# Another order of units in the mixers of a two-block decoder, and half of the low parts moved to VectorE

## Chip, core and metric

The kernel runs on one core of one Trainium2 chip. The metric is the device time of one execution in microseconds (us), lower is better. TensorE does the matrix products, VectorE, ScalarE and GpSimd the elementwise work, SyncE issues the weight loads. In the profile they are PE, DVE, ACT, POOL and SP.

## What is computed

Input is one sequence of 512 positions of width 1024. Two blocks follow each other. The first holds two attention layers (one with a forget gate, one with a sliding window of 128 and sinks). The second block, in which the change lies, is cut here to its core:

```python
h = rmsnorm_2(x, norm_mix_w) * (1.0 + sc1) + sh1
proj = h @ w_in
(hq, hf, hi, hg, sq, sk, sv, iq, ik, iw, cu) = split(proj)
o_a = hgrn2_mixer(hq, hf, hi, hg, lower_bounds, onorm_w)   # 4 heads, 128 x 128, gated linear recurrence
o_b = dsa_mixer(sq, sk, sv, iq, ik, iw)                    # 4 heads of 64, softmax over the 128 best keys
o_c = conv_module(cu, cv_w, cv_b, ln_w, ln_b)              # gated, 31 taps over positions, layer norm, swish
x = x + g1 * (concatenate([o_a, o_b, o_c]) @ w_out)
h = rmsnorm_2(x, norm_mlp_w) * (1.0 + sc2) + sh2
x = x + g2 * (square(relu(h @ mlp_w1)) @ mlp_w2)
return rmsnorm_2(x, final_norm_w)
```

All of it is in float32. The three mixers `hgrn2_mixer`, `dsa_mixer` and `conv_module` depend on nothing of each other until the product with `w_out`.

## The kernel before

**Products.** Positions lie in four tiles of 128. A float32 product is three products of a reduced format (`mm3`, L270 to L275): every operand is a high part and a low part. A weight group is 1024 x 512, loaded in four quarters `raw` of 128 x 1024 (`load_group`, L248 to L268; the pool has three `raw` buffers, so the load of a quarter waits until the one three before it is done with). ScalarE writes the high part `wh` (L259), and the low part `wl = raw - wh` comes from GpSimd for the quarters listed in `gpl` and from VectorE otherwise (L259, recorded at helper line L115). A product over a quarter needs both.

**Units.** The mixers are emitted by a hand-written list of units, `ORDER` (L1160), one word each; words that repeat run a generator from one `yield` to the next. The words: `iq` and `sv` project the indexer's queries and the sparse values (groups narrower than 512); `s1` to `s3` are indexer scores of a position tile (`score`, L833: eight products `Si`, each ReLU on ScalarE, then a sum `sct` on VectorE), `t1` to `t3` select the 128 best keys (`select`, L852: 16 MAX and 15 MATCH_REPLACE rows on VectorE, then the mask `posm`); `f0`, `f1` and `v0`, `v1` are gates (`hg_gates`, L908) and values (`hg_values`, L935: products `pshi`, gate `thg`) for heads 0 and 1 or 2 and 3; `h0` to `h3` are the four linear-recurrence heads (`hg_head`, L956); `cu` and `c0`, `c1` are the convolution's projection and its two halves (`u_cv`, L1119: one row and 30 taps `cv` each on VectorE); `sqk` projects the sparse queries and keys; `d0`, `d1` are the two pairs of sparse-attention heads (`u_dsa`, L1111, with `fox_pair`); `ln` is the convolution's layer norm.

**A head.** `hg_head` multiplies halves of ever longer runs of positions: a first block product, `D`, and nine levels (`lev` 0 to 8). A level is a product `psA` on TensorE, a masked copy into `D` on VectorE (L998, levels 0 to 5), and then doubling (L980): `qv` times `prod` or `kG` on VectorE, `kG` times `prod` on GpSimd, before the next level's product. Each needs the one before. Then come the output product `Oh`, a normalisation with a root on GpSimd (`hhr`), ScalarE's scaling `on`, a transpose `pth` and the mixer output `xm`.

**What sets the order.** Words are emitted in the order of the list; a static scheduler then fixes one instruction order per engine at build time, taking earlier words first where several instructions could run. On the chip each engine works through its list in order and waits by semaphore. Buffers are shared by tag: seven of 128 x 512 (`w2`, used by `rsi`, `E`, `sg`, `prod`, `D`, `gt`, `eq`, `pre` and more), three banks `mm` for large products, two `ss` for `Si`, `psA` and the sparse scores `S`.

Behind the list, `residual` (L638) multiplies the mixer outputs with `wo2`.

Of the kernel before, what the change touches and what calls it, by code (L numbers as in the profile page):

```python
# [64 lines left out]
def decoder_kernel(ctx: ExitStack, tc: tile.TileContext, a: dict, out: bass.AP, upto="all"):  # L65
# [750 lines left out]
    levm = const.tile([128, 6, 64], U8, name="levm")  # L816
    ve.tensor_copy(levm, levf.rearrange("p (l j) -> p l j", j=64))

    gpc = [int(x) for x in "0123"]
    gpo = [int(x) for x in "0"]  # L820
    cnt[1] = int("1000")
    LAG = "v"
# [334 lines left out]
            stt(zz, th, 1.0, zz, ALU.add, ALU.mult)  # L1157
            mix_out(1, 2 + m, zz, 0.5)

    ORDER = "iq sv s2 s3 f0 f0 f0 s1 v0 v0 t2 f1 f1 f1 cu h1 h1 t3 h0 h1 h0 c1 sqk h1 h0 t1 sqk h0 v1 d1 d1 d1 d1 d1 d0 v1 d0 d0 d0 c0 h2 h2 h2 ln h3 d0 h3 h3 h2 h3".split()  # L1160
    gens = {}

    def unit(w):
# [10 lines left out]

    for w in ORDER:
        k, n = w[0], int(w[1]) if w[1].isdigit() else None
# [222 lines left out]
```

## Time and profile before

| | |
|---|---|
| Time, median of 3 runs | 1336.72 us (1330.08 to 1338.33) |
| The profiled execution | 1335.75 us, span 1334.0 us |
| TensorE busy, whole span | 1232.4 us (92%) |
| VectorE busy, whole span | 819.5 us (61%) |
| ScalarE busy, whole span | 550.6 us (41%) |
| GpSimd busy, whole span | 312.0 us (23%) |
| Low parts on VectorE, whole span | 104 of 128 x 1024, 129.7 us |
| Low parts on GpSimd, whole span | 34, 76.4 us |

Times in the trace count from the start of the span. The mixers lie between about 646 and 931. A row of the timeline gives start, duration, engine, line, operation, the tile written and the tiles read, and in brackets how long the engine was idle ahead of it and which instruction ended that. A stretch's busy time counts an instruction that is held up on the way as busy.

### The profile page before, as it was taken

What the parts mean: (1) busy time and instruction counts of PE and PEld (TensorE: products, weight loads), DVE (VectorE), ACT (ScalarE), POOL (GpSimd) and SP (SyncE); (2) the same over time, 40 slices, a digit from 0 to 9 for tenths busy, and PEclk for the clock granted to TensorE, in tenths of its full rate; (3) what the DMA queues carried; (4) which work ended last, traced back from release to release, by engine and by line L of the source; (5) the groups of instructions that cost most, each with busy time, mean ns of one, the idle gap of its engine ahead of it and who ended that gap; (6) DMA issues with size and microseconds to landing.
All of it is one profiled execution on the core that took longest, in us unless ns stands there. A gap on an engine that the chain in (4) does not pass through costs nothing.

```text
span 1334.0 us, 17842 instructions
## 1 busy us (share of the span) xinstructions
PE 1232.4 (92%) x6596; PEld 1008.0 (76%) x6596; DVE 819.5 (61%) x1598; ACT 550.6 (41%) x1144; POOL 312.0 (23%) x362
## 2 busy tenths in 40 slices
PE   5999998999999989999988896878999999999997
PEld 4677777878886878888776665766788888888886
DVE  4647656756467678545699979863675244353444
ACT  4544453554255657526433134613352322131222
POOL 1304302210124240003335634142111010015211
PEclk9999999999999889999999999888999999999999
DMA  5234324423532343252322302120364233234221
GB/s 200 66 112 142 127 81 157 143 66 126 204 107 69 95 142 127 66 182 93 98 67 79 111 1 67 48 80 17 110 206 158 89 117 108 82 116 153 95 79 64
DMA packets 42023, 141.72 MB, mean 106 GB/s; under 512 B 4928, under 2 KB 5824, under 8 KB 41936
## 3 DMA queue, kind: packets, MB, share of 16 engines
q1 hardware_dynamic: 36144, 126.06, 29.2%
q10 hardware_dynamic: 5792, 14.52, 3.1%
q8 instruction: 52, 0.85, 0.3%
q14 instruction: 35, 0.29, 0.1%
HBM read 132.14 MB, written 8.42 MB: 105 GB/s over the span
## 4 chain that ended last, share of the span: by engine, by line
PE 54%; DVE 11%; issue 8%; POOL 6%; DMA 2%; ACT 2%; POOLq 0%; SPq 0%; ACTq 0%; DVEq 0%
PE psw L275 4%; PE psw L274 4%; PE psw L273 4%; PE psf L275 4%; PE psf L274 4%; PE psf L273 4%; POOL wl L115 3%; PE pso L274 2%; PE pso L273 2%; PE pso L275 2%; DVE cv L118 2%; PE psg L275 2%; PE psg L274 2%; PE psg L273 2%; PE Ob L743 2%
## 5 line engine op out<-in xcount | busy, mean ns | idle before, releaser
L259 ACT ACTIVATE wh<-raw 128x1024 fp32r<-128x1024 f32 (+2 forms) x138 | 142.3, 1037 | 164.8 <-PE psw L275 50.5
L115 DVE TENSOR_TENSOR wl<-raw,wh 128x1024 fp32r<-128x1024 f32 x104 | 129.7, 1260 | 58.5 <-ACT wh L259 56.3
L115 POOL TENSOR_TENSOR wl<-raw,wh 128x1024 fp32r<-128x1024 f32 (+2 forms) x34 | 76.4, 2264 | 83.0 <-ACT wh L259 82.9
L274 PE MATMUL psf<-xfl,wh 128*128 128x512 f32 (+1 forms) x232 | 85.4, 369 | 0.5 <-DVE xfl L118 0.5
L275 PE MATMUL psf<-xfh,wl 128*128 128x512 f32 (+1 forms) x232 | 85.3, 368 | 0.3 <-DVE wl L115 0.2
L115 POOL TENSOR_TENSOR hnr<-hnr,mhalf 128x8 f32<-128x8 f32 (+1 forms) x28 | 49.6, 1771 | 153.5 <-DVE hnr L111 148.2
L273 PE MATMUL psf<-xfh,wh 128*128 128x512 f32 (+1 forms) x232 | 84.5, 368 | 0.0
L1239 POOL TENSOR_SCALAR acth<-sqf 128x512 fp32r<-128x512 f32 x32 | 22.9, 718 | 242.3 <-DVE sqf L115 242.3
L273 PE MATMUL psw<-wh,acth 128*128 128x512 f32 (+1 forms) x206 | 79.0, 383 | 0.0
L275 PE MATMUL psw<-wh,actl 128*128 128x512 f32 (+1 forms) x206 | 78.9, 383 | 0.0
L274 PE MATMUL psw<-wl,acth 128*128 128x512 f32 (+1 forms) x206 | 78.9, 383 | 0.0
L519 ACT ACTIVATE PT<-ptp 128x512 f32<-128x512 f32 (+3 forms) x96 | 45.5, 481 | 43.0 <-PE ptp L548 30.2
L336 DVE CUSTOM_DVE_ANT_0 adaw<-adaw,cact 128x1024 f32<-128x1024 f32 x48 | 58.1, 1225 | 7.1 <-DMA adaw<-in_ada 6.9
L511 ACT ACTIVATE P<-Sp,nm 128x128 f32<-128x128 f32 (+3 forms) x80 | 44.5, 557 | 28.2 <-DVE nm L509 27.9
L118 DVE SCALAR_TENSOR_TENSOR cv<-glu,cols,cv 128x482 f32<-128x482 f32 (+29 forms) x60 | 55.5, 930 | 0.4
L273 PE MATMUL psq<-wh,xah 128*128 128x512 f32 x128 | 54.0, 422 | 0.8 <-ACT xah L294 0.8
L275 PE MATMUL psq<-wh,xal 128*128 128x512 f32 x128 | 53.4, 417 | 0.2 <-DVE xal L115 0.2
L274 PE MATMUL psq<-wl,xah 128*128 128x512 f32 x128 | 52.8, 413 | 0.0
L275 PEld LDWEIGHTS psf<-xfh,wl 128*128 128x128 f32 x232 | 43.7, 188 | 8.2 <-DVE wl L115 1.1
L274 PEld LDWEIGHTS psf<-xfl,wh 128*128 128x128 f32 x232 | 43.7, 188 | 8.1 <-DVE xfl L118 0.9
L273 PEld LDWEIGHTS psf<-xfh,wh 128*128 128x128 f32 x232 | 43.5, 188 | 7.3
L554 PEld LDWEIGHTS O<-v,PT 128*128 128x128 f32 x320 | 42.8, 193 | 7.5 <-ACT PT L519 5.1
(501 smaller groups left out, 3471.5 us busy)
## 6 DMA issues: line engine op xcount, KB each, us to landing
raw<-in_w SPq DMA_DIRECT2D x56, 512.0 KB, 3.7
adaw<-in_ada SPq DMA_DIRECT2D x48, 512.0 KB, 4.2
raw<-in_wa SPq DMA_DIRECT2D x32, 512.0 KB, 4.6
raw<-in_w2m SPq DMA_DIRECT2D x32, 512.0 KB, 4.0
raw<-in_wb SPq DMA_DIRECT2D x16, 512.0 KB, 4.7
ck<-cd ACTq DMA_DIRECT2D x16, 256.0 KB, 4.1
raw<-in_woa SPq DMA_DIRECT2D x8, 512.0 KB, 4.7
raw<-in_wob SPq DMA_DIRECT2D x8, 512.0 KB, 4.7
```

The lines of the kernel that those rows point to most:

```text
L115: return note(eng, eng.tensor_tensor(o, x, y, op=op))
L118: return note(ve, ve.scalar_tensor_tensor(o, x, s, y, op0=op0, op1=op1, **kw))
L259: i = ac.activation(wh, r, AF.Copy), tt(gp if len(res) in (gpa if gpl is None else gpl) else ve, wl, r, wh.bitcast(F32), ALU.subtract)
L273: te.matmul(o, lh, rh, start=i == 0, stop=False)
L274: te.matmul(o, lh, rl, start=False, stop=False)
L275: te.matmul(o, ll, rh, start=False, stop=i == n - 1)
L336: i = ve.tensor_tensor_reduce(w, w, ada["c"], 1.0, 0.0, op0=ALU.mult, op1=ALU.add, accum_out=mod[:, j:j + 1])
L511: ac.activation(P[:, :n], Sp[:, :n], AF.Exp, bias=nm, scale=-1.0, accum_out=l)
L519: ac.activation(o, i, AF.Copy)
L554: te.matmul(O[:, i, s], PT[s][:, j], v[:, j, (2 * p + s) * 64:(2 * p + s + 1) * 64], start=j == 0, stop=j == i)
L743: te.matmul(O[:, i, s], PTs[s, kb][:, i], vb[:, n - nkb + 1 + kb, g * 64:g * 64 + 64], start=kb == 0, stop=kb == nkb - 1)
L1239: gp.tensor_scalar(xh, s, 1.0, 0.0, op0=ALU.mult, op1=ALU.add)
```

## The change

Two constants. `gpc` is the `gpl` of all eight weight groups of the mixers: quarters 0 and 2 stay on GpSimd, quarters 1 and 3 go to VectorE. `ORDER` lists the same words (the same units, each as often as it has pieces) in another order.

```diff
-    gpc = [int(x) for x in "0123"]
+    gpc = [int(x) for x in "02"]
...
-    ORDER = "iq sv s2 s3 f0 f0 f0 s1 v0 v0 t2 f1 f1 f1 cu h1 h1 t3 h0 h1 h0 c1 sqk h1 h0 t1 sqk h0 v1 d1 d1 d1 d1 d1 d0 v1 d0 d0 d0 c0 h2 h2 h2 ln h3 d0 h3 h3 h2 h3".split()
+    ORDER = "iq sv s2 s1 f0 f0 f0 v0 v0 t2 h1 s3 f1 h0 f1 f1 t1 cu h0 c1 sqk h1 h1 h0 h0 sqk h1 t3 v1 d1 d0 d1 d1 d1 c0 d0 d0 v1 h2 d0 h2 h3 ln h2 h3 h2 d0 h3 d1 h3".split()
```

What this does to the engines' lists is shown at three places. The first is VectorE at the end of the first value group and the selection of tile 2 (`gt`, `eq`, `pre` of scores `sct_6195`). Before:

```order
L868 TENSOR_SCALAR gt_6672,cg_6675<-sct_6195,m8_6670 128x384
L118 SCALAR_TENSOR_TENSOR thg_6620<-thg_6620,pshi_6594 128x256
L111 TENSOR_SCALAR eq_6673<-sct_6195,m8_6670 128x384
L112 TENSOR_SCALAR need_6679<-cg_6675 128x1
L862 MAX m8_7070<-sct_6239 128x8
L870 SCALAR_TENSOR_TENSOR pre_6674<-ones1_106,eq_6673 128x384
L864 MATCH_REPLACE sct_6239<-m8_7070,sct_6239 128x512
L118 SCALAR_TENSOR_TENSOR eq_6673<-pre_6674,need_6679,eq_6673 128x384
L862 MAX m8_7073<-sct_6239 128x8
L115 TENSOR_TENSOR gt_6672<-gt_6672,eq_6673 128x384
L864 MATCH_REPLACE sct_6239<-m8_7073,sct_6239 128x512
```

Now:

```order
L868 TENSOR_SCALAR gt_6628,cg_6631<-sct_6195,m8_6626 128x384
L118 SCALAR_TENSOR_TENSOR thg_6576<-thg_6576,pshi_6550 128x256
L111 TENSOR_SCALAR eq_6629<-sct_6195,m8_6626 128x384
L112 TENSOR_SCALAR need_6635<-cg_6631 128x1
L115 TENSOR_TENSOR qv_6308<-qv_6308,kG_6307 128x512
L870 SCALAR_TENSOR_TENSOR pre_6630<-ones1_106,eq_6629 128x384
L115 TENSOR_TENSOR D_6650<-psA_6652,idc_5849 128x256
L118 SCALAR_TENSOR_TENSOR eq_6629<-pre_6630,need_6635,eq_6629 128x384
L998 COPY_PREDICATED D_6650<-levm_5851,psA_6663 128x256
L115 TENSOR_TENSOR gt_6628<-gt_6628,eq_6629 128x384
L115 TENSOR_TENSOR qv_6308<-qv_6308,kG_6307 128x256
L115 TENSOR_TENSOR wl_6762<-raw_6759,wh_6761 128x1024
```

The first rows and levels of head 1 (`D`, `qv`) now stand in that selection, where rows of the next selection stood, and the fourth low part of the second gate group (`wl_6762`) follows on VectorE.

The second place is the loading of the second value group (`raw_7616` to `raw_7634`, unit `v1`). Before, all four of its low parts stood on GpSimd:

```order
L115 TENSOR_TENSOR hhr_7398<-hhr_7398,mhalf_104 128x4
L115 TENSOR_TENSOR kG_6307<-kG_6307,prod_7117 128x128
L115 TENSOR_TENSOR wl_7619<-raw_7616,wh_7618 128x1024
L115 TENSOR_TENSOR wl_7625<-raw_7622,wh_7624 128x1024
L115 TENSOR_TENSOR wl_7631<-raw_7628,wh_7630 128x1024
L115 TENSOR_TENSOR wl_7637<-raw_7634,wh_7636 128x1024
```

Now the second and fourth stand on VectorE, here:

```order
L118 SCALAR_TENSOR_TENSOR cv_7174<-glu_7031,cols_84,cv_7174 128x509
L115 TENSOR_TENSOR qv_6308<-qv_6308,prod_6801 128x128
L118 SCALAR_TENSOR_TENSOR cv_7174<-glu_7031,cols_84,cv_7174 128x510
L864 MATCH_REPLACE sct_6697<-m8_7587,sct_6697 128x512
L118 SCALAR_TENSOR_TENSOR cv_7174<-glu_7031,cols_84,cv_7174 128x511
L862 MAX m8_7590<-sct_6697 128x8
L115 TENSOR_TENSOR wl_7625<-raw_7622,wh_7624 128x1024
L115 TENSOR_TENSOR on_7411<-Oh_7400,gg_6433 128x512
L864 MATCH_REPLACE sct_6697<-m8_7590,sct_6697 128x512
L115 TENSOR_TENSOR wl_7637<-raw_7634,wh_7636 128x1024
```

They follow the last of the 30 taps of one half of the convolution (`cv`, 511 columns), among which the last levels of heads 0 and 1 (`qv`) and the selection of tile 3 (`sct_6697`) are spread.

The third place is VectorE behind the last tap. `D_8084` and `D_8036` belong to head 2, `D_8266` and `D_8177` to head 3; `qv_6709` and `qv_6766` hold the queries of both. Before, the end of head 2 and the start of head 3:

```order
L115 TENSOR_TENSOR qv_6709<-qv_6709,kG_6708 128x512
L112 TENSOR_SCALAR ct_8189<-ptc_8190,bmv_8205,rrcr_8207 128x256
L112 TENSOR_SCALAR ct_8189<-ptc_8211,bmv_8218,rrcr_8220 128x256
L1144 BN_STATS bst_8224<-ptc_8211 128x6
L115 TENSOR_TENSOR qv_6709<-qv_6709,kG_6708 128x256
L1146 BN_AGGR bmv_8226<-bst_8224 128x2
L111 TENSOR_SCALAR rrcr_8228<-bmv_8226 128x1
L112 TENSOR_SCALAR ct_8189<-ptc_8211,bmv_8226,rrcr_8228 128x256
L118 SCALAR_TENSOR_TENSOR zz_8237<-th_8239,zz_8237 128x512
L115 TENSOR_TENSOR D_8266<-psA_8268,idc_5849 128x256
```

Now:

```order
L998 COPY_PREDICATED D_8036<-levm_5851,psA_8133 128x256
L115 TENSOR_TENSOR qv_6766<-qv_6766,prod_8026 128x32x8
L559 RECIPROCAL rl8f_8121<-l8f_7729 128x8
L115 TENSOR_TENSOR onf_8123<-O_7728,rl8f_8121 128x512
L998 COPY_PREDICATED D_8036<-levm_5851,psA_8145 128x256
L115 TENSOR_TENSOR qv_6766<-qv_6766,prod_8026 128x16x16
L1144 BN_STATS bst_8230<-ptc_8225 128x6
L1146 BN_AGGR bmv_8232<-bst_8230 128x2
L115 TENSOR_TENSOR xm_7867<-O_7728,xm_7866 128x512
L998 COPY_PREDICATED D_8036<-levm_5851,psA_8157 128x256
L115 TENSOR_TENSOR D_8177<-psA_8179,idc_5849 128x256
L115 TENSOR_TENSOR qv_6766<-qv_6766,kG_6765 128x512
```

Head 3's `D` stood behind all nine levels of head 2 and the layer norm's tiles `ct`; it now stands behind head 2's level 5, and the end of a sparse pair (`onf_8123`, `xm_7867`) stands ahead of it, behind the last tap.

## Rows read from the trace of the kernel before

**Rows 1.** Busy time by stretch, mixers; columns in the first line.

```profile
core 0: us, PE busy (x) PEld busy (x) DVE busy (x) ACT busy (x) POOL busy (x), PEclk, DMA share, GB/s
646.20:758.30 112.10, 99.17 (x426) 76.47 (x426) 108.93 (x195) 41.79 (x66) 50.26 (x34) 0.98 0.26 81
758.30:833.20 74.90, 57.59 (x448) 44.60 (x447) 64.64 (x109) 25.40 (x62) 36.38 (x39) 0.94 0.18 52
833.20:880.10 46.90, 41.78 (x268) 34.61 (x269) 39.14 (x78) 24.44 (x64) 11.22 (x17) 0.91 0.26 87
880.10:931.40 51.30, 40.03 (x329) 30.53 (x328) 23.16 (x56) 15.43 (x45) 16.83 (x28) 0.85 0.02 8
```

**Rows 2.** Timeline, TensorE, 823.6 to 834; start, us, line, tiles, [idle before, releaser].

```profile
823.62 0.40 PE L273 MATMUL pshi<-wh,xch 128*128 128x512 f32 x1
823.85 0.40 PE L274 MATMUL pshi<-wl,xch 128*128 128x512 f32 x1
...
833.74 0.77 PE L1038 MATMUL pth<-ident,on 128*128 128x128 f32 x2 [9.50 <-ACT on L1035]
```

**Rows 3.** Groups by form, VectorE, 640-930; busy us, mean ns, idle us before.

```profile
L118 DVE SCALAR_TENSOR_TENSOR sct<-rsi,siw,sct 128x384 f32<-128x384 f32 x7 | 8.2, 1172 | 0.7
...
L111 DVE TENSOR_SCALAR kG<-sg 128x512 f32<-128x512 f32 x4 | 6.4, 1589 | 0.0
...
L118 DVE SCALAR_TENSOR_TENSOR kG<-E,oml,sg 128x512 f32<-128x512 f32 x4 | 5.2, 1290 | 0.0
...
L115 DVE TENSOR_TENSOR wl<-raw,wh 128x1024 fp32r<-128x1024 f32 x3 | 3.6, 1215 | 0.0
...
L118 DVE SCALAR_TENSOR_TENSOR cv<-glu,cols,cv 128x503 f32<-128x503 f32 x2 | 1.5, 739 | 0.0
```

**Rows 4.** Timeline around the second value group's low parts: GpSimd, then VectorE.

```profile
804.94 10.71 POOL L115 TENSOR_TENSOR wl<-raw,wh 128x1024 fp32r<-128x1024 f32 x4 [1.92 <-ACT wh L259]
...
804.99 2.88 DVE L118 SCALAR_TENSOR_TENSOR cv<-glu,cols,cv 128x494 f32<-128x494 f32 x1
...
808.39 2.25 DVE L118 SCALAR_TENSOR_TENSOR cv<-glu,cols,cv 128x495 f32<-128x495 f32 x1
...
810.62 5.56 DVE L118 SCALAR_TENSOR_TENSOR cv<-glu,cols,cv 128x482 f32<-128x482 f32 x2
```

**Rows 5.** Timeline, VectorE, ahead of the first score row.

```profile
645.83 0.17 DVE L111 TENSOR_SCALAR siw<-psv 128x8 f32<-128x8 f32 x1 [3.45 <-ACT svw L1052]
```

**Rows 6.** Timeline at the first low part of `wo2`'s second half: GpSimd, then VectorE.

```profile
937.92 2.41 POOL L115 TENSOR_TENSOR wl<-raw,wh 128x1024 fp32r<-128x1024 f32 x1 [9.93 <-ACT wh L259]
...
938.35 2.53 DVE L115 TENSOR_TENSOR hres<-gm,hres 128x512 f32<-128x512 f32 x1
```

**Rows 7.** VectorE timeline, level products of heads 0, 1: first and last wait.

```profile
769.83 0.45 DVE L998 COPY_PREDICATED D<-levm,psA 128x256 f32<-128x256 uint8 x1 [1.84 <-PE psA L977]
...
786.98 0.37 DVE L115 TENSOR_TENSOR qv<-qv,prod 128x128 f32<-128x128 f32 x1 [0.89 <-PE psA L1008]
```

**Rows 8.** Timeline, VectorE, last taps to last mixer output.

```profile
878.57 1.52 DVE L118 SCALAR_TENSOR_TENSOR cv<-glu,cols,cv 128x510 f32<-128x510 f32 x2
...
881.90 0.45 DVE L998 COPY_PREDICATED D<-levm,psA 128x256 f32<-128x256 uint8 x1 [0.91 <-PE psA L977]
...
883.83 0.44 DVE L998 COPY_PREDICATED D<-levm,psA 128x256 f32<-128x256 uint8 x1
...
902.77 0.42 DVE L115 TENSOR_TENSOR D<-psA,idc 128x256 f32<-128x256 f32 x1
...
920.33 0.31 DVE L115 TENSOR_TENSOR qv<-qv,prod 128x128 f32<-128x128 f32 x1 [1.33 <-PE psA L1008]
...
930.66 0.69 DVE L115 TENSOR_TENSOR xm<-pth,xm 128x512 fp32r<-128x512 f32 x1 [3.76 <-ACT xm L901]
```

**Rows 9.** Busy time by stretch, instructions on the low parts `wl` alone.

```profile
646.20:931.40 285.20, 87.55 (x213) 41.71 (x214) 3.64 (x3) 59.88 (x24) 0.94 0.19 61
```

**Rows 10.** Busy time by stretch, behind TensorE's longest wait (columns as in rows 1).

```profile
830.00:840.00 10.00, 6.26 (x26) 5.01 (x27) 8.25 (x21) 5.37 (x21) 2.85 (x3) 0.60 0.05 13
```

## The prediction

> **What bounds the kernel now.** I read three views for this. First the busy time by stretch, over the mixers only: from the first score row on VectorE (646.2) to the last mixer output (931.4). The profiled execution took 1335.75 us around a span of 1334.0; the mixers are 285.2 of it, and the change touches nothing else that weighs. Summed over the four stretches TensorE is busy 238.6 us there, VectorE 235.9 [rows 1]. The whole-kernel share (TensorE 92%, VectorE 61%) says "TensorE"; the stretches say something else. VectorE is busy 108.93 of 112.1 us, then 64.64 of 74.9, then 39.14 of 46.9, up to the last tap of the depthwise convolution at 880.1. So for 234 us VectorE's queue has only 21.2 us of idle time. In the last 51.3 us it is busy for 23.16 only: there a chain of short steps sets the pace [rows 1].
>
> Second, the waits. TensorE's longest one in the mixers, 9.5 us, is a transpose behind a ScalarE step [rows 2]; that step waits for a GpSimd root, which waits for two tiny VectorE rows that stand among the taps. VectorE's lateness, again.
>
> Third, what VectorE's time consists of. One tap of 503 columns takes 0.74 us [rows 3]. While GpSimd works through the four low parts of one weight group (10.7 us), four taps take 2.88, 2.25 and 5.56 (two) [rows 4]. Other rows that read only SBUF swell in the same way under the other groups [rows 3]. A low part on GpSimd is thus not free for VectorE: it stops it.
>
> So until the last tap the end is set by VectorE's queue (its work, its blocked time, its idle time), and after it by the level chains of heads 2 and 3.
>
> **The change part by part: the low parts.** Of 32 low parts on GpSimd, the second and fourth of each group of four move: 16. Four are the narrow ones of `iq` and `sv`, before 646, where VectorE waits up to 3.45 us for ScalarE between its rows [rows 5]; they cost nothing there, and without that cover 4 x 0.7 = 2.8 us (the wide one's time scaled by width). Twelve are 128x1024 at 1.215 us [rows 3]. One of them stands ahead of the first score row, and two of the three old ones of `wo2` slip behind the last tap, so the queue up to the last tap gains 12 - 1 - 2 = 9, **+10.9 us**.
>
> What leaves is blocking. Lower bound from the form means, against a tap's 0.739: seven score rows 7 x (1.172 - 0.739), the two kinds of `kG` row 4 x (1.589 - 0.739) + 4 x (1.290 - 0.739), and the four taps 10.69 - 2.96 [rows 3, 4]. That is 3.0 + 5.6 + 7.7 = 16.3 us over 24 low parts, 0.68 each; 0.739 is too long for the narrower rows, and further forms swell that I have not listed, so the truth is higher. Upper bound: 7.7 / 4 = 1.9, as under the taps. I take 1.1, since only one group in six runs beside taps. Twelve leave: **-13.2 us** (bounds -8 and -23).
>
> The two halves can also block each other. The nearest row is a residual addition that took 2.53 us beside a low part on GpSimd, where a row of its width takes 0.69 [rows 6, 8]: 1.85 us per meeting. That is what the 1.1 already contains for any instruction; I add one more meeting than average, **+2** (bounds 0 and 12 x 1.85 = 22).
>
> **The order, up to the last tap.** Before, heads 0 and 1 ran their levels when nothing else was in VectorE's queue: eight waits for level products between 769.8 and 787.0 (1.84, 2.41, 0.93, 0.95, 0.87, 0.36, 0.35, 0.89) make 8.6 us; the first and the last of the eight are in [rows 7]. Now their first levels stand among selection and gate rows and the rest among the taps, as the order rows show, so something stands between each product and its use: **-8.6**. New waits: the shifts of `sqk`'s third part now wait for transposes that stand on TensorE behind a head's output. I allow **+2**. Bounds for both together: 0 and -21.2, all idle time. Last, the two widest masked minima of a sparse pair and its scaled output and mixer output now stand behind the last tap instead of ahead of it: four rows of 512 columns, taken at a mixer output's 0.69 [rows 8], and 0.3 for three tiny ones: **-3.1**.
>
> Sum to the last tap: 10.9 - 13.2 + 2 - 8.6 + 2 - 3.1 = -10.0, so it ends near 870.
>
> **The order, behind the last tap.** Before, head 3's first row comes at 902.77, 22.7 us after the last tap, since all nine levels of head 2 and the convolution's normalisation stand ahead; from there to the last output (930.66 + 0.69) are 28.6 us [rows 8]. Now head 3 starts when head 2 has done level 5. The pitch of a level is 1.9 us (881.90, 883.83 [rows 8]): five levels 9.5, two low parts 2.4, two masked minima 1.4, together 13.3; I take 14. Behind it head 3 needs its nine levels (17.1) and the 11 us from its last level row (920.33) to its output [rows 8], 28.1, and shares the queue with head 2's three last levels and the normalisation; I take 31. So 45 instead of 51.3: **-6.3** (bounds 0 and -8.7).
>
> **Sum:** -10.0 - 6.3 = -16.3; 1335.75 - 16.3 = **1319 us**. The median of the runs is 1336.72, so that is 1.3% under it. TensorE has 238.6 us of work for 269 us; it fits, if not with much to spare.
>
> **The rivals.**
> *The halves exclude each other (slower).* Each low part on VectorE becomes ready one ScalarE copy after GpSimd's, so it could find GpSimd in the middle of its own. Then VectorE's whole queue stands for up to 2.5 us (59.88 / 24 [rows 9]) each time: 12 x 2.5 - 2 = +28. And the relief then stays at its lower bound, -8 instead of -13.2, since GpSimd's halves block as before and for longer: +5. 1319 + 28 + 5 = **1352**. The point from which it decides: with the relief at -8 the sum is 1324, and the old time is passed at (1335.75 - 1324) / 2.5, so with five meetings more than I allowed; all twelve put it over 1%. Against it: VectorE's queue is late, not waiting for its parts, so most of its halves come after GpSimd's are over. The Trainium skill's page SBUF — State Buffer, section "Who interferes with whom", has a rule that speaks for this rival: a VectorE instruction with two SBUF inputs and a GpSimd instruction that reads SBUF use one shared read interface, and whoever comes second stands still until the other is through. The trace agrees as far as one meeting shows it (2.53 against 0.69, [rows 6, 8]); how many of the twelve meet, the page cannot say.
>
> *TensorE starved at the second value group (no change).* Its second low part now stands behind 30 taps, so only 15 of the first 96 products of that kind are done ahead of the sparse attention, where before 57 were. 42 x 0.23 (823.62, 823.85 [rows 2]) = 9.7 us have to fit into a stretch where TensorE had 46.9 - 41.78 = 5.1 idle [rows 1]. At worst the whole 9.7 is paid: **1329**.
>
> *The tap end alone does not move (no change).* If the waits filled come back elsewhere (0 for the -8.6) only the net low parts and the tail remain: 1319 + 8.6 + 2 = **1330**. For it: a queue in fixed order finds another product to wait for.
>
> *More comes off (faster still).* The granted clock is 0.60 in 830 to 840, behind the 9.5 us wait [rows 2, 10]: a mean between the two levels, most of the stretch at the lower one (1.2 of 2.4 GHz). With that wait gone the 10 us at 0.60 give back up to 4, and all 21.2 of idle time might be filled: 1319 - 4 - 8 = **1307**.
>
> **How the numbers follow.** The forecast 0.45, starved 0.20, waits come back 0.10, more 0.12, halves exclude 0.13. A measurement can tell about 1% (13.4 us) here from no change: the bounds are 1323 and 1350. Faster holds the case in which more comes off and three quarters of the forecast with a little of the starved case (0.12 + 0.34 + 0.02 = 0.48); slower is most of the excluding halves (0.10), whose lesser forms fall within 1%; same is the rest, 0.42. The range from 1304 to 1341 leaves out the worse half of the excluding halves above and the end of the best case below. The forecast's own range is 1311 to 1327.
>
> **What would show it.** Right: VectorE's taps at about 0.74 outside two instead of four swollen ones per group; the last tap near 870; no 9.5 us transpose wait; head 3's first row some 14 us behind the last tap. Wrong: low parts on VectorE of 2 to 3.7 us (halves exclude); level products on TensorE waiting for VectorE rows that stand behind taps, and value products still running beside the last level chain (starved); VectorE idle above 15 us before the last tap.

## The result and the profile after

The changed kernel takes 1315.74 us (median of 4 runs, 1312.96 to 1322.57) against 1335.48 for the kernel before: a ratio of 0.9865, 95% interval 0.9839 to 0.9891. A second comparison, beside three of the experiments below, gives 0.9863 (0.9838 to 0.9888). That is 18 us less; the forecast was 16.3 less. The profiled execution took 1312.96 us, its span is 1311.1 (before 1334.0); the difference of the two spans, 22.9 us, is larger than that of the medians, so readings of the trace carry an error of a few us.

Busy time by stretch, changed kernel, from the first score row on VectorE to the last mixer output; the second cut at 861.07 is the end of the last convolution tap:

```profile
core 0: us, PE busy (x) PEld busy (x) DVE busy (x) ACT busy (x) POOL busy (x), PEclk, DMA share, GB/s
645.30:750.50 105.20, 96.29 (x510) 74.67 (x509) 101.08 (x192) 39.17 (x63) 35.75 (x36) 0.98 0.25 82
750.50:812.00 61.50, 49.78 (x301) 38.72 (x300) 57.45 (x95) 20.78 (x39) 18.19 (x18) 0.92 0.19 61
812.00:861.07 49.07, 41.43 (x276) 34.48 (x276) 46.24 (x97) 29.04 (x82) 14.83 (x20) 0.99 0.11 35
861.07:908.53 47.46, 42.50 (x378) 32.41 (x374) 27.91 (x65) 18.92 (x52) 17.09 (x29) 0.94 0.20 72
```

Against [rows 1]: the mixers last 263.2 us instead of 285.2. Up to the last tap they take 215.8 instead of 233.9; VectorE's idle time there is 11.0 us (215.8 less 101.08, 57.45 and 46.24) instead of 21.2. Behind the last tap they take 47.5 instead of 51.3. TensorE's busy time is 230.0 instead of 238.6, at a higher granted clock.

VectorE's groups by form of the changed kernel, from 645 to 909 (busy us, mean ns, idle before):

```profile
L115 DVE TENSOR_TENSOR wl<-raw,wh 128x1024 fp32r<-128x1024 f32 x15 | 23.9, 1590 | 2.2 <-ACT wh L259 2.2
L115 DVE TENSOR_TENSOR qv<-qv,prod 128x256 f32<-128x256 f32 x24 | 12.9, 536 | 0.8 <-PE psA L1003 0.8
L998 DVE COPY_PREDICATED D<-levm,psA 128x256 f32<-128x256 uint8 x24 | 10.6, 440 | 4.8 <-PE psA L977 4.7
L118 DVE SCALAR_TENSOR_TENSOR sct<-rsi,siw,sct 128x384 f32<-128x384 f32 x7 | 4.3, 616 | 0.5
L118 DVE SCALAR_TENSOR_TENSOR kG<-E,oml,sg 128x512 f32<-128x512 f32 x4 | 3.5, 868 | 0.0
L111 DVE TENSOR_SCALAR kG<-sg 128x512 f32<-128x512 f32 x4 | 3.2, 796 | 0.0
```

The score rows fell from 1172 ns to 616, the two `kG` rows from 1589 and 1290 to 796 and 868 [rows 3]. Most of them no longer stand beside GpSimd's low parts; one `kG` row of 1.95 us and one of 1.24 still do. But a low part on VectorE has a mean of 1590 ns, not 1215: three of the fifteen met one on GpSimd. One meeting, GpSimd's row and then VectorE's:

```profile
670.52 2.48 POOL L115 TENSOR_TENSOR wl<-raw,wh 128x1024 fp32r<-128x1024 f32 x1 [0.31 <-ACT wh L259]
...
670.69 3.40 DVE L115 TENSOR_TENSOR wl<-raw,wh 128x1024 fp32r<-128x1024 f32 x1
```

VectorE's row takes 3.40 us: its own 1.21 and 2.2 in which it stands still until GpSimd is through (the other two took 2.58 and 3.35). GpSimd's row, which began first, is not longer for it. Where GpSimd's row begins inside VectorE's it is longer, as at the meeting ahead of the first score row:

```profile
642.74 2.58 DVE L115 TENSOR_TENSOR wl<-raw,wh 128x1024 fp32r<-128x1024 f32 x1 [2.24 <-ACT wh L259]
...
644.18 3.38 POOL L115 TENSOR_TENSOR wl<-raw,wh 128x1024 fp32r<-128x1024 f32 x1
```

VectorE behind the last tap, changed kernel:

```profile
860.33 0.74 DVE L118 SCALAR_TENSOR_TENSOR cv<-glu,cols,cv 128x511 f32<-128x511 f32 x1
860.99 1.21 DVE L115 TENSOR_TENSOR wl<-raw,wh 128x1024 fp32r<-128x1024 f32 x1
...
863.00 1.21 DVE L115 TENSOR_TENSOR wl<-raw,wh 128x1024 fp32r<-128x1024 f32 x1
...
874.70 0.41 DVE L115 TENSOR_TENSOR D<-psA,idc 128x256 f32<-128x256 f32 x1
...
907.84 0.69 DVE L115 TENSOR_TENSOR xm<-pth,xm 128x512 fp32r<-128x512 f32 x1 [3.87 <-ACT xm L901]
```

Head 3's first row comes 13.6 us behind the last tap (874.70 less 861.07) instead of 22.7 [rows 8].

TensorE's longest waits in the mixers of the changed kernel:

```profile
701.80 0.69 PE L977 MATMUL psA<-qv,kG 128*64 128x64 f32 x16 [4.07 <-DVE qv L115]
...
761.47 1.12 PE L977 MATMUL psA<-qv,kG 128*64 128x64 f32 x16 [4.13 <-DVE qv L115]
...
823.75 0.62 PE L1038 MATMUL pth<-ident,on 128*128 128x128 f32 x2 [0.87 <-ACT on L1035]
...
860.55 1.12 PE L977 MATMUL psA<-qv,kG 128*64 128x64 f32 x16 [4.33 <-DVE qv L115]
```

The transpose that waited 9.5 us [rows 2] waits 0.87 now. The three longest that are left, of about 4 us, are each for a head's level row `qv` on VectorE.

So the forecast's size held. Whether its reasons did is a matter of taking the change apart.

### The profile page after: what moved, and what is told of

It is laid out like the page before. It is cut to its first block, busy times and chain, and to the rows that moved or that the text cites. A ratio compares the mean times of both kernels' runs of the same rounds, so it can differ in the third digit from the quotient of the medians.

```text
span 1311.1 us, 17809 instructions
## 1 busy us (share of the span) xinstructions
PE 1222.6 (93%) x6596; PEld 1000.8 (76%) x6596; DVE 820.0 (63%) x1614; ACT 551.5 (42%) x1144; POOL 276.7 (21%) x346
## 4 chain that ended last, share of the span: by engine, by line
PE 57%; DVE 14%; issue 4%; DMA 3%; POOL 3%; ACT 2%; POOLq 0%; SPq 0%; ACTq 0%; DVEq 0%
PE psw L273 4%; PE psw L275 4%; PE psw L274 4%; PE psf L275 4%; PE psf L273 4%; PE psf L274 4%; PE pso L274 3%; PE pso L275 3%; PE pso L273 3%; PE psg L275 2%; PE O L554 2%; PE psg L274 2%; PE psg L273 2%; DVE cv L118 2%; DVE wl L115 2%
## 5 line engine op out<-in xcount | busy, mean ns | idle before, releaser
L115 DVE TENSOR_TENSOR wl<-raw,wh 128x1024 fp32r<-128x1024 f32 (+2 forms) x120 | 153.6, 1293 | 65.1 <-ACT wh L259 62.9
L1239 POOL TENSOR_SCALAR acth<-sqf 128x512 fp32r<-128x512 f32 x32 | 22.9, 717 | 242.2 <-DVE sqf L115 242.2
L115 POOL TENSOR_TENSOR wl<-raw,wh 128x1024 fp32r<-128x1024 f32 (+2 forms) x18 | 40.2, 2240 | 88.1 <-ACT wh L259 88.1
```

The costliest lines, as they stand in the source:

```text
L115: return note(eng, eng.tensor_tensor(o, x, y, op=op))
L1239: gp.tensor_scalar(xh, s, 1.0, 0.0, op0=ALU.mult, op1=ALU.add)
```

## The experiments

Three theories were weighed. The first, close to the forecast's, has two causes that add: filled waits (order and tail, some 17 us) and a small net gain of the low parts (2 to 4 us; 0.3 in the forecast's sum). Its rivals are that the order is everything, and that the low parts are. All times below are ratios to the kernel before, run on the same chip (medians 1333 to 1335 us), so 0.1% is 1.3 us. For orientation, all readings first. The four columns at the right are from each profiled execution, in us after the first score row: the end of the last tap, the end of the last product of the second value group on TensorE (`pshi`, unit `v1`), the start of head 3's first row `D` on VectorE, and the end of the last mixer output.

| kernel | ratio (95% interval) | last tap | last `pshi` | head 3 begins | end |
|---|---|---|---|---|---|
| before | 1 | 233.9 | 211.1 | 256.6 | 285.1 |
| changed | 0.9865 (0.9839 to 0.9891) | 215.8 | 202.0 | 229.4 | 263.2 |
| order alone | 1.0009 (0.9991 to 1.0026) | 215.6 | 221.2 | 251.6 | 285.4 |
| halves alone | 0.9915 (0.9893 to 0.9937) | 215.8 | 206.8 | 245.9 | 273.8 |
| tail alone | 0.9944 (0.9923 to 0.9964) | 232.5 | 211.1 | 243.0 | 276.7 |
| halves and tail | 0.9903 (0.9878 to 0.9929) | 216.6 | 206.7 | 236.4 | 270.3 |
| changed, old tail | 0.9935 (0.9913 to 0.9956) | 214.8 | 202.0 | 248.2 | 276.1 |
| changed, late groups on GpSimd | 0.9977 (0.9961 to 0.9993) | 220.7 | 215.5 | 247.6 | 281.4 |
| changed, early groups on GpSimd | 0.9922 (0.9896 to 0.9948) | 223.8 | 218.3 | 241.2 | 275.1 |
| changed, `v1` on GpSimd | 0.9912 (0.9893 to 0.9930) | 220.7 | 205.0 | 237.0 | 270.8 |
| changed, all on VectorE | 0.9880 (0.9860 to 0.9900) | 216.3 | 197.8 | 234.8 | 268.7 |
| changed, one of four on GpSimd | 0.9880 (0.9860 to 0.9899) | 208.2 | 195.9 | 232.8 | 266.7 |
| changed, the other two quarters | 0.9918 (0.9894 to 0.9941) | 219.1 | 215.4 | 242.6 | 276.6 |

### The order alone

From the changed kernel:

```diff
-    gpc = [int(x) for x in "02"]
+    gpc = [int(x) for x in "0123"]
```

> The changed kernel with all four low parts of each mixer weight group back on GpSimd: the new order alone. My theory (two causes that add: filled waits by the order, relief from GpSimd's blocking by the low parts): the trace of the changed kernel shows 10 us less idle time on VectorE up to the last tap, 3 us of rows moved behind it, 4 us in the tail, so about 17 us without relief: near 1318. Rival 1 (the order is everything, each low part on VectorE costs as much as its blocking on GpSimd): 1314 to 1316, as the changed kernel. Rival 2 (the low parts are everything): 1333 to 1337, as before.

Measured: 1334.93 us, ratio 1.0009. The new order alone brings nothing; the forecast's largest term falls with it. Where it went shows in two groups of VectorE's rows. First before, then the order alone:

```profile
L115 DVE TENSOR_TENSOR qv<-qv,prod 128x256 f32<-128x256 f32 x24 | 14.3, 600 | 2.0 <-PE psA L1003 2.0
L998 DVE COPY_PREDICATED D<-levm,psA 128x256 f32<-128x256 uint8 x24 | 10.7, 445 | 16.3 <-PE psA L977 16.1
```

```profile
L115 DVE TENSOR_TENSOR qv<-qv,prod 128x256 f32<-128x256 f32 x24 | 23.3, 969 | 2.3 <-PE psA L1003 2.3
L998 DVE COPY_PREDICATED D<-levm,psA 128x256 f32<-128x256 uint8 x24 | 10.6, 442 | 8.0 <-PE psA L977 7.8
```

The idle time ahead of the level copies `D` falls from 16.3 to 8.0 us, and all of VectorE's idle time up to the last tap from 21.2 to 12.3: the waits are filled, as forecast (8.6 less 2 of new ones). But the level rows `qv` grow from 14.3 to 23.3, by 9.0; five of the 24, of 2.23 to 2.60 us, carry it. In this order the levels of heads 0 and 1 stand beside low parts on GpSimd, and a level row reads only SBUF. GpSimd, VectorE and TensorE of the order alone at one such place:

```profile
768.22 2.33 POOL L115 TENSOR_TENSOR wl<-raw,wh 128x1024 fp32r<-128x1024 f32 x1
...
768.27 0.43 DVE L998 COPY_PREDICATED D<-levm,psA 128x256 f32<-128x256 uint8 x1
768.61 2.23 DVE L115 TENSOR_TENSOR qv<-qv,prod 128x256 f32<-128x256 f32 x1
...
770.98 1.12 PE L977 MATMUL psA<-qv,kG 128*64 128x64 f32 x16 [6.36 <-DVE qv L115]
```

The level row takes 2.23 us instead of the 0.41 of such a row standing free (changed kernel, 760.91), and the next level product waits 6.36 us for it (in the changed kernel 4.13). Not all of that is the level row: two taps ahead of it in VectorE's queue, beside other low parts, take 2.24 and 2.15 us. Each level of a head needs the one before, so these delays add up along the head: the last output row `on` of heads 0 and 1 begins 189.5 us after the first score row, 172.0 in the changed kernel. The second value group's products end 221.2 us after it, against 202.0. The waits of VectorE became blocked time of VectorE, and on a longer chain.

This also breaks the forecast's picture of what sets the end. The last tap lies 18 us earlier than before (215.6 against 233.9), and the time has not moved: 69.8 us remain behind it. The last tap is not the hinge. Head 3's first row and the last mixer output of the order alone:

```profile
894.75 0.41 DVE L115 TENSOR_TENSOR D<-psA,idc 128x256 f32<-128x256 f32 x1
...
927.89 0.69 DVE L115 TENSOR_TENSOR xm<-pth,xm 128x512 fp32r<-128x512 f32 x1 [3.87 <-ACT xm L901]
```

The table shows what does go with the end. From head 3's first row to the last output every kernel with the new tail takes 33.7 to 34.0 us, and every kernel with the old tail 27.8 to 28.6. So the end follows the moment at which head 3 can begin, and in the order alone that is 22 us later than in the changed kernel.

### The halves alone

From the kernel before:

```diff
-    gpc = [int(x) for x in "0123"]
+    gpc = [int(x) for x in "02"]
```

> The kernel before with the second and fourth low part of each mixer weight group on VectorE: the old order, the low parts alone. My theory: 12 more low parts at 1.21 us are 14.6 us of work less what leaves as blocking, about 17 us: a gain of 2 to 4, near 1332. Rival 1 (order is everything): 1335. Rival 2 (low parts are everything): 1316. A third reading (the halves meet GpSimd's in the old order, 2 us each, six times or more): 1340 and above.

Measured: 1321.85 us, ratio 0.9915, 11 us less, where the forecast's terms give about nothing (10.9 - 13.2 + 2). It fits none of the theories: too much for mine, too little for the rival that the low parts are everything. VectorE's groups, old order with halves:

```profile
L115 DVE TENSOR_TENSOR wl<-raw,wh 128x1024 fp32r<-128x1024 f32 x15 | 25.0, 1667 | 2.2 <-ACT wh L259 2.2
...
L118 DVE SCALAR_TENSOR_TENSOR sct<-rsi,siw,sct 128x384 f32<-128x384 f32 x7 | 4.3, 617 | 0.5
L111 DVE TENSOR_SCALAR kG<-sg 128x512 f32<-128x512 f32 x4 | 3.3, 823 | 0.1
L118 DVE SCALAR_TENSOR_TENSOR kG<-E,oml,sg 128x512 f32<-128x512 f32 x4 | 3.0, 742 | 0.0
...
L998 DVE COPY_PREDICATED D<-levm,psA 128x256 f32<-128x256 uint8 x24 | 10.7, 444 | 8.5 <-PE psA L977 8.4
```

Summed over all forms of a tile in the mixers, what shrank against before is: taps 8.1 us, score and selection rows `sct` 5.5, `kG` 5.3, `eq` 3.9, `qv` 1.5, together 24.3. For twelve low parts that is 2.0 each, where the forecast took 1.1 out of bounds of 0.68 and 1.9. A low part on GpSimd costs VectorE most of the 2.4 us that it runs; one on VectorE costs 1.21 and, when it meets the other half, up to 2.2 more.

This relief alone does not make the 11 us: the rows `wl` on VectorE take 21.4 us more (25.0 against 3.6), so some 3 us are left of it. The waits fell as well, in the old order: the idle time ahead of the level copies `D` from 16.3 to 8.5 us, and all of VectorE's idle time up to the last tap from 21.2 to 13.3. The order alone brought it to 12.3, both together to 11.0. Order and halves thus shorten VectorE's idle time by nearly the same amount, and together hardly by more than either. How the halves do it was not taken apart.

The trace also shows TensorE's wait at the second value group:

```profile
805.27 0.39 PE L273 MATMUL pshi<-wh,xch 128*128 128x512 f32 x1
817.25 0.80 PE L274 MATMUL pshi<-wl,xch 128*128 128x512 f32 x1 [11.59 <-DVE wl L115]
```

That is the forecast's rival "TensorE starved at the second value group", 11.6 us long, in the old order: the low part stands behind a run of taps, and the product that needs it is the next in TensorE's list.

### The tail alone

From the kernel before, only the end of the list (its front is as before and not shown):

```diff
-    ORDER = "... v1 d1 d1 d1 d1 d1 d0 v1 d0 d0 d0 c0 h2 h2 h2 ln h3 d0 h3 h3 h2 h3".split()
+    ORDER = "... v1 d1 d1 d1 d1 d0 v1 d0 d0 c0 h2 d0 h2 h3 ln h2 h3 h2 d0 h3 d1 h3".split()
```

> The kernel before with only the last part of the list of units in the new order (heads 2 and 3 interleaved, the ends of the sparse pairs among them). My theory: the stretch behind the last tap shrinks by 4 to 6 us and a sparse pair's end leaves the queue ahead of it (3 us) only to come back behind it: 1330 to 1332. Rival (the tail was not what ended last, or loses as much to the two chains sharing VectorE): 1335.

Measured: 1326.62 us, ratio 0.9944, 7.5 us less. Busy time up to the last tap and behind it:

```profile
645.84:878.37 232.53, 194.13 (x1109) 152.85 (x1110) 211.10 (x372) 88.53 (x185) 96.89 (x88) 0.93 0.22 71
878.37:922.51 44.14, 41.00 (x350) 31.20 (x350) 24.27 (x62) 19.02 (x52) 15.95 (x28) 0.96 0.06 21
```

The stretch behind the last tap is 44.1 us; 45 were forecast from the pitch of a level. This term was right, and the gain is larger than the 2 to 4 us expected of this run: the rows of the sparse pair that moved behind the tap are paid for within the 44.1. TensorE, which works through two heads in place of one, runs there at a granted clock of 0.96 instead of 0.85 [rows 1].

### Do halves and tail make up the whole?

The two alone give 11.3 + 7.5 = 18.8 us, all that the change gives. If they add, the middle of the list (heads among scores and gates) is worth nothing. Two kernels ask this: the kernel before with halves and new tail, and the changed kernel with the old tail.

The first, from the kernel before:

```diff
-    gpc = [int(x) for x in "0123"]
+    gpc = [int(x) for x in "02"]
-    ORDER = "... v1 d1 d1 d1 d1 d1 d0 v1 d0 d0 d0 c0 h2 h2 h2 ln h3 d0 h3 h3 h2 h3".split()
+    ORDER = "... v1 d1 d1 d1 d1 d0 v1 d0 d0 c0 h2 d0 h2 h3 ln h2 h3 h2 d0 h3 d1 h3".split()
```

> The kernel before with half of the low parts on VectorE and with the new last part of the list, the middle of the list as before. Theory A (halves and tail are the whole gain and add up; heads beside scores and gates bring nothing of their own): 11 + 8 us off, near 1315, as the changed kernel. Theory B (the new middle matters once the halves are in: it keeps the second value group's products from waiting 11.6 us for a low part behind taps, as they do with the old middle, and so lets heads 2 and 3 start): the tail cannot start earlier than those products end, so near 1322, as the halves alone.

The second, from the changed kernel:

```diff
-    ORDER = "... d0 d0 v1 h2 d0 h2 h3 ln h2 h3 h2 d0 h3 d1 h3".split()
+    ORDER = "... d0 d0 v1 d1 d0 h2 h2 h2 ln h3 d0 h3 h3 h2 h3".split()
```

> The changed kernel with heads 2 and 3 and the ends of the sparse pairs in the old sequence at the end of the list. Theory A (the interleaved tail is worth what it is worth alone): plus 6 to 8, near 1323. Theory B (the tail overlaps here with other work that has to be done behind the last tap anyway): plus 0 to 3, 1316 to 1319.

Measured: halves and tail 1322.24 us, ratio 0.9903, hardly better than the halves alone (0.9915, the intervals overlap). The old tail in the changed kernel 1324.82, ratio 0.9935, so there the tail is worth 0.7%, 9 us. With the halves in, then, the tail gains 9 us with the new middle and next to nothing with the old one; with the old middle and no halves it had gained 7.5. In the kernel with halves and tail TensorE's wait is still there:

```profile
815.21 0.80 PE L274 MATMUL pshi<-wl,xch 128*128 128x512 f32 x1 [11.57 <-DVE wl L115]
```

Its last value product comes 206.7 us after the first score row, in the changed kernel at 202.0. In the changed kernel those products too come to a stop (from 794.57 to 808.83 none runs), but level and output products of heads 0 and 1 stand there and fill part of it (TensorE is busy for 6.80 of the 10 us from 800). Head 3 begins 7 us earlier there (229.4 against 236.4). What the middle of the list brings in time is 0.9903 against 0.9865 and 0.9863, some 5 us. The intervals overlap (0.9878 to 0.9891), so this one difference is likely, not certain.

### Which low parts block the new order

From the changed kernel, the groups of `cu`, `sqk` and `v1`:

```diff
-        w = load_group(a["w2"][3 + 2 * hh], gpl=gpc)
+        w = load_group(a["w2"][3 + 2 * hh], gpl=[0, 1, 2, 3] if hh else gpc)
...
-        wc = load_group(a["w2"][1], gpl=gpc)
+        wc = load_group(a["w2"][1], gpl=[0, 1, 2, 3])
...
-        wqk = load_group(a["w2"][0], gpl=gpc)
+        wqk = load_group(a["w2"][0], gpl=[0, 1, 2, 3])
```

> The changed kernel with all four low parts on GpSimd in the convolution's group, the sparse queries' and keys' and the second value group (the late groups), halves as they are in the other groups. Theory C (the new order alone loses its gain because these low parts stand on GpSimd beside the levels of heads 0 and 1: level rows on VectorE stop for 2 us each, and the next product, the second value group and heads 2 and 3 are late): 15 or more of the 18 us are lost, 1330 or above. Rival D (each of the low parts weighs the same): half of it, near 1325.

From the changed kernel, both gate groups and the first value group:

```diff
-        w = load_group(a["w2"][2 + 2 * hh], gpl=gpc)
+        w = load_group(a["w2"][2 + 2 * hh], gpl=[0, 1, 2, 3])
...
-        w = load_group(a["w2"][3 + 2 * hh], gpl=gpc)
+        w = load_group(a["w2"][3 + 2 * hh], gpl=gpc if hh else [0, 1, 2, 3])
```

> The changed kernel with all four low parts on GpSimd in both gate groups and the first value group (the early groups), halves as they are in the later ones. Theory C (the late groups beside the levels matter): a few us at most, 1316 to 1320. Rival D (each low part weighs the same): near 1325.

Measured: late groups 1330.44, ratio 0.9977, 15 us of the gain lost; early groups 1324.00, ratio 0.9922, 8 us lost. Six low parts move in either. So where they stand matters (the late ones, beside the levels of heads 0 and 1, weigh twice), but the early ones weigh more than my theory allowed. The two losses add to 23 us, more than the 19 that the order alone lies above the changed kernel: they overlap.

### The second value group, and how many on each engine

From the changed kernel, the second value group only:

```diff
-    w = load_group(a["w2"][3 + 2 * hh], gpl=gpc)
+    w = load_group(a["w2"][3 + 2 * hh], gpl=[0, 1, 2, 3] if hh else gpc)
```

> The changed kernel with the second value group's four low parts on GpSimd; all else as changed. Rival of the prediction (TensorE starved at the second value group, because its second and fourth low parts stand behind taps on VectorE): a gain of up to 10 against the changed kernel, 1306 to 1313. My theory (GpSimd's two extra low parts stop taps or level rows for about 2 us each, and save 2 x 1.2 on VectorE): 0 to plus 5, 1316 to 1321.

Measured: 1322.67 us, ratio 0.9912: 6.5 us slower than the changed kernel, a little beyond what my theory gave, and the opposite of the rival. GpSimd, VectorE and TensorE of this kernel, at the second and third low part of the group, which now follow each other on GpSimd:

```profile
792.49 5.09 POOL L115 TENSOR_TENSOR wl<-raw,wh 128x1024 fp32r<-128x1024 f32 x2
...
792.58 2.80 DVE L118 SCALAR_TENSOR_TENSOR cv<-glu,cols,cv 128x500 f32<-128x500 f32 x1
...
795.63 2.50 DVE L118 SCALAR_TENSOR_TENSOR cv<-glu,cols,cv 128x501 f32<-128x501 f32 x1
...
798.60 1.08 PE L1003 MATMUL psA<-qv,kG 128*64 128x64 f32 x8 [5.57 <-DVE qv L115]
```

Two taps take 2.80 and 2.50 us instead of 0.73, with a level row queued behind them; TensorE then waits 5.57 us for it.

The other variants of the count start from the changed kernel too. None on GpSimd:

```diff
-    gpc = [int(x) for x in "02"]
+    gpc = [int(x) for x in ""]
```

> The changed kernel with all low parts of the mixers on VectorE, none on GpSimd. My theory (a low part on GpSimd costs VectorE about what it costs to do it there: 12 us still lost by taps beside GpSimd and 5.7 us by three swollen low parts, against 12 more at 1.21 us = 14.6): a gain of 0 to 5 against the changed kernel, 1311 to 1316. Rival (VectorE's queue is the bound by its count of work, blocking is hidden in waits): plus 14, near 1330.

One of four:

```diff
-    gpc = [int(x) for x in "02"]
+    gpc = [int(x) for x in "0"]
```

> The changed kernel with only the first low part of each mixer group on GpSimd, three on VectorE. If a low part on GpSimd costs VectorE about 2 us of stop and a low part done there 1.2: minus 5, near 1311. If the two are even, as all four on VectorE (1318) suggests: 1315 to 1319.

The other two:

```diff
-    gpc = [int(x) for x in "02"]
+    gpc = [int(x) for x in "13"]
```

> The changed kernel with the other two quarters on GpSimd (second and fourth; first and third on VectorE). The same number on each engine. If only the count matters: 1314 to 1318. If it matters which meets what: the products over the first quarter wait for VectorE's queue instead of GpSimd's, so TensorE starts each group later where VectorE is behind: plus 3 to 8, 1319 to 1324.

And the changed kernel itself, once more, beside these:

> The changed kernel once more, beside the variants of this call and the kernel before: 1314 to 1318, or 0.984 to 0.989 of before. It tells whether it lies clear of halves and tail alone (0.9903), which would make the new middle of the list worth something.

Measured: none on GpSimd 1318.05 (0.9880; a little above the 1311 to 1316 of my theory), one of four 1316.85 (0.9880), two of four 1314.07 (0.9863): the same within the intervals. From four to two the gain is 19 us (1.0009 to 0.9865); from two to none there is none. With none on GpSimd VectorE is busy for 5.7 us less in the mixers (227.0 against 232.7), but idle for longer up to the last tap (16.9 us against 11.0). The other two quarters, as many on each engine, give 1324.64 (0.9918), 7 us worse than the first and third: it matters which. What it is there is not settled. The trace of that kernel shows other waits, among them 2.84 us of TensorE for a head's `prod` on GpSimd, and the value products end at 215.4; but no run takes these causes apart.

No variant beats the changed kernel.

## Why the prediction was right, step by step

The time (1319 forecast, 1315.74 measured) and the range (1304 to 1341) held. Of the steps, these did:

- **The tail.** 45 us forecast behind the last tap; 44.1 with the tail alone, 47.5 in the changed kernel. Head 3's first row 14 us behind the last tap; 13.6. From there to the end 31 were forecast; 33.8. The gain of 6.3 is measured as 7.5 alone and 9 within the change.
- **The count of low parts.** Nine more up to the last tap, as counted. The `wl` rows in VectorE's queue take 18.95 - 3.64 = 15.3 us more there: the 10.9 of the sum and 4.4 for two meetings, where the sum had 2. The two cost 2.2 and 2.1; with the one ahead of the first score row they are three of fifteen, far from the rival's twelve.
- **The filled waits, as such.** VectorE's idle time up to the last tap fell by 10.2 us; 8.6 less 2 were forecast, and the order alone fills 8.9. But the halves alone fill 7.9, which no term of the forecast held.
- **The wait of 9.5 us** is gone.

These did not:

- **"Until the last tap the end is set by VectorE's queue."** The order alone, the halves alone and both together put the last tap at the same place, 215.6 to 215.8 us, and end 285.4, 273.8 and 263.2 us after the first score row. So "the last tap near 870" missed too: it came at 861.07, 18.1 us less from the first score row where the sum had 10.0. What the three differ in is the tail and the moment at which head 3 begins (251.6, 245.9, 229.4), in the same sequence as the last product of the second value group on TensorE (221.2, 206.8, 202.0). The value products alone do not set it: with no low part on GpSimd they end at 197.8, earlier than in the changed kernel, and head 3 begins at 234.8, later. On TensorE head 2's first level products stand among the last products of the sparse pairs; what holds heads 2 and 3 in each case was not taken apart.
- **"8.6 us of waits filled" as a gain of its own.** The forecast put that term beside the blocking as if they were independent. They are not. A wait that is filled puts another row there, and if a low part runs on GpSimd at that time, a row that reads only SBUF, as a level row does, stops. With all low parts on GpSimd the order gave 8.3 us of idle time back as 9.0 us of swollen level rows, and gained nothing.
- **The relief, 1.1 us for each low part.** 24.3 / 12 = 2.0 in the old order, just above the upper bound of 1.9. The lower bound was made of the forms that I had listed; the forms not listed (`eq` and `qv` rows, score rows of other widths, further taps) held the rest. In the changed kernel, against before, the same sum is 16.9 (`sct` 5.3, `kG` 4.9, `eq` 4.6, `qv` 2.1) with nothing from the taps, since there the halves left on GpSimd run beside taps: the tap rows sum to 57.0 us before and 56.9 after, where I had looked for two swollen ones in place of four in a group.
- **The clock.** I had given it up to 4 us, as part of a rival. TensorE's busy time in the mixers is 8.6 us shorter for the same products; the granted clock went from 0.94 to 0.96 on average, and some of the 8.6 is records missing from the trace (1455 matmuls against 1468).

So errors of both signs met, and that the sum came near is in good part luck: alone, the order is worth 17 us less than its terms (8.6 - 2 + 3.1 + 6.3 = 16.0 forecast, 1.2 lost), the halves 11 more. Together they are worth 18, by an interplay of 8 us that no term held: order and halves alone add to 1.2 - 11.3 = -10.1 us. The order brings its gain only where the low parts do not stop the level rows: the order alone and the late groups show that. That the halves bring theirs in full only where TensorE has level products left for the time that the second value group waits is argued from one difference whose intervals overlap.

Of the rivals, *the halves exclude each other* has its mechanism (3.40 us in one meeting) at a quarter of the count. The rule of the Trainium skill's page SBUF — State Buffer, section "Who interferes with whom", that the later of the two stands still, agrees with the rows (3.40 us against 1.21, and 2.23 against 0.41 for a level row), and it bears on the level rows as much as on the halves. *TensorE starved* is real with the old middle (11.6 us) and paid only partly with the new. *Waits come back elsewhere* fits the order alone, and I had given it 0.10. *More comes off* has the direction of the clock right, but its sum is wrong: to fill all 21.2 us of idle time is 14.6 beyond the forecast's 8.6 less 2, not 8, so its best case was near 1300, below the stated range.

## What to carry to other kernels

Idle time that an order fills is a gain only if the rows that move there run at their own speed: look first at what runs on the engine that shares a path with them. Before two edits are priced as a sum, ask whether one changes the price of the other; a run of each alone takes little and here turned the explanation round. And test a supposed hinge (a last tap) by a kernel that moves it and nothing else.

## What the hardware showed

A GpSimd row that subtracts two 128x1024 operands in SBUF mostly takes 2.33 to 2.5 us here, 3.38 where it came second to a low part on VectorE. Most VectorE rows with all operands in SBUF that begin inside it stand still until it is through. A row with one tensor input and a scalar does not escape: the first row of a tap run takes 2.32 us beside it and 0.47 without. MAX and MATCH_REPLACE of 256 columns do escape: they take 0.43 and 0.41 inside it, as they do in the kernel with no low part on GpSimd. So does a level copy `D`, with one operand in PSUM (0.43 at 768.27 of the order alone). GpSimd's row first, then VectorE's, changed kernel:

```profile
752.05 2.41 POOL L115 TENSOR_TENSOR wl<-raw,wh 128x1024 fp32r<-128x1024 f32 x1 [17.00 <-ACT wh L259]
...
752.42 2.32 DVE L111 TENSOR_SCALAR cv<-glu,cols 128x512 f32<-128x512 f32 x1
...
761.25 0.47 DVE L111 TENSOR_SCALAR cv<-glu,cols 128x512 f32<-128x512 f32 x1
```

```profile
692.73 2.41 POOL L115 TENSOR_TENSOR wl<-raw,wh 128x1024 fp32r<-128x1024 f32 x1
...
692.93 0.41 DVE L864 MATCH_REPLACE8 sct<-m,sct 128x256 f32<-128x256 f32 x1
693.37 0.43 DVE L862 MAX8 m<-sct 128x8 f32<-128x256 f32 x1
```

And a stall of TensorE can be paid twice. Behind the 5.57 us wait in the kernel with `v1` on GpSimd the granted clock is 0.50, the lower of the two levels (1.2 of 2.4 GHz), and value products start every 0.43 us; a little later it is 1.00, and they start every 0.23. TensorE alone (us, busy, clock, DMA share, GB/s):

```profile
799.62:803.20 3.58, 3.58 (x9) 0.50 0.21 85
803.78:805.40 1.62, 1.62 (x10) 1.00 0.24 53
```

In the same way the granted clock is 0.50 in and behind the end of the 11.6 us wait of the halves alone, and 0.67 on average behind the wait of 4.33 us of the changed kernel. First the halves alone, then the changed kernel (columns as in [rows 1]):

```profile
810.00:820.00 10.00, 1.22 (x2) 0.50 (x2) 9.68 (x15) 2.74 (x6) 5.34 (x5) 0.50 0.00 0
```

```profile
860.00:870.00 10.00, 7.30 (x72) 5.68 (x72) 7.82 (x16) 3.43 (x7) 2.35 (x3) 0.67 0.59 204
```

How much of the 18 us is clock and how much is waiting was not taken apart; what the trace gives is 8.6 us of TensorE's busy time and 13.4 of its idle time, out of 22.0 in the mixers of the two profiled executions.
